# The norm of the last two tokens taken apart from its half, with their residual sums in four column groups

## The chip, the cores and the metric

One core of a Trainium2 chip runs the whole program. The metric is the device time of one execution in microseconds (us). The kernel before has a median of 1541.15 us over three runs (1540.23 to 1541.41).

## The reference

A block with a token mixer and a gated channel mixer, for 1024 tokens behind 16 learned ones (T = 1040), model width 1024, 2816 inner channels, all in float32:

```
h = concat(meta, x)
h = h + token_mixer(rmsnorm(h, norm_mix_g))        # eight heads, then "mixed @ w_out"
u = rmsnorm(h, norm_ffn_g)
h = h + (silu(causal_dwconv(u @ w_up)) * (u @ w_gate)) @ w_down
out = rmsnorm(h, norm_final_g)[:, 16:]

def rmsnorm(x, g):
    return x * rsqrt(mean(x * x, axis=-1) + EPS) * g
```

The mixer is four mLSTM heads and four retention heads, each worked in chunks of tokens with a state that is carried on.

## The kernel before, in words

Activations lie channel by token: `resid` has 128 partitions, 8 blocks of channels and 1040 columns (tokens). Every float32 product is made of three matmuls of 32-bit "fp32r" operands: each operand is split into `hi` (a rounded copy, on ACT) and `lo` (the rest, on DVE), and hi·hi, hi·lo and lo·hi are added in PSUM. Lines 394 to 396, 404 to 406 and 577 to 579 are such triples. A scheduler of the framework turns the program text into one fixed order for each engine, and each engine then works strictly in that order; dependences between engines are semaphore waits. PSUM has eight banks, handed out by tags: `pp` (3), `sA` (2), `num`, `upd` and `tr` (1 each).

**Heads.** `ORDER` puts head 4 (`HF`) first. For each head `o_group` makes the gates, then `v_group` of the next head runs chunk by chunk while the scan of this head (`scan_a`, `scan_b`) is woven in. Weights come through `need(key, ahead)`, which loads and splits units in a fixed sequence: v, v, q, k, o, o of one head, then of the next. `ahead` says how many units further the split is issued; line 442 asks for 4 in the second half of `o_group`, so the next head's q weights are split (lines 162 and 163, `hi_q` on ACT, `lo_q` on DVE) from there. For q units the split is ordered behind the latest evacuation of a v chunk (`last["v"]`). The raw weights have a ring of two buffers.

**The output projection.** `mixw` multiplies by `w_out` with a seven-product scheme over steps named 1, 65, 73, 4 and 2. It covers columns 14 to 1037. The last two tokens (columns 1038 and 1039) are kept apart: DVE accumulates their product in `acc` (`last_two`), with channels along the free dimension, as partial sums over 128 partitions. Inside step 4, line 1216 sums them over the partitions and turns them to channel by token: 16 matmuls, one for each channel block and token, with a piece of `acc` as weights and one column of ones as the moving operand. Line 1217 adds the result to `resid`.

**The norms behind it.** `norm_tasks` squares each channel block (line 1122, ACT), sends the block to a DRAM copy (`stream`, line 1124, SP) and adds the squares up in `Rb` (line 1126, DVE). `rms` sums over the partitions (line 314, PE, tile `pcb`), takes root and reciprocal (lines 319 and 320) and spreads the factor to all partitions (line 325, PE, `prb`); line 329 (ACT) copies it to `Rb`. `scale_tasks` multiplies `resid` by it (line 1136, DVE) and writes the split operands `xh` and `xl` (lines 1064 and 1065). The second half of the tokens, columns 526 to 1039, is one unit of 514 columns (`BQ`), so its squares stand behind line 1217. Its norm has one sum bank and one broadcast bank, both of tag `tr`; as 514 is two more than four times 128, it has a small group of two columns and four of 128.

**Step 2 and the quarters.** Step 2 fills four banks `pwy` for the first quarter of the tokens; line 736 (DVE) adds each to `resid`. Then the same four banks are filled for the second quarter, with operands `wl`; each of these starts when line 736 has read its bank. Behind them come the first up and gate products (`first_up`, `first_gate`, tiles `pup` and `pga`), the second half of the tokens first.

Of the kernel before, what the change touches and what calls it, by code (L numbers as in the profile page):

```python
# [10 lines left out]
F32 = mybir.dt.float32  # L11
# [52 lines left out]
def body(ctx, tc, h_in, vecs, cst, mask_in, rot, w_v0, w_v, w_fm, w_out, w_up, w_gate, w_down, out):  # L64
# [46 lines left out]
    def pp(name, tag="pp"):  # L111
        return ps.tile([P, 512], F32, tag=tag, name=name, bufs=PSB[tag])
# [193 lines left out]
    def rms(ss, t0, t1, nm, col, rb, ptags=("tr", "num"), more=(), sq=None):  # L306
        n = t1 - t0
        o = n % P
        subs = ([(0, o)] if o else []) + [(i, P) for i in range(o, n, P)]
        ns = len(subs)  # L310
        pc = rps("pc" + nm, ptags[0])
        for i, (o, w) in enumerate(subs):
            for a in (ss, *more):
                nc.tensor.matmul(pc[:w, i:i + 1], a[:, o:o + w], cs[:, C_M01 + P - 1:C_M01 + P], start=a is ss, stop=a is (ss, *more)[-1])
        i0 = 1 if subs[0][1] < P else 0
        for w, j0, j1 in ([(subs[0][1], 0, 1)] if i0 else []) + [(P, i0, ns)]:
            if sq is not None:
                nc.vector.tensor_scalar(sq[:w, j0:j1], pc[:w, j0:j1], 1.0 / D, EPS, ALU.mult, ALU.add)
            nc.scalar.activation(col[:w, j0:j1], pc[:w, j0:j1], AF.Sqrt, bias=epsc[:w], scale=1.0 / D)
            nc.vector.reciprocal(col[:w, j0:j1], col[:w, j0:j1])  # L320
        pr = rps("pr" + nm, ptags[1])
        x = max(0, n - 512)
        for i, (o, w) in enumerate(subs):
            dst = pr[:, o - x:o - x + w] if o >= x else pc[:, 8:8 + w]
            nc.tensor.matmul(dst, col[:w, i:i + 1].to_broadcast([w, P]), ident[:w, :w], start=True, stop=True)
        if x:
            nc.scalar.copy(rb[:, :x], pc[:, 8:8 + x])
        if rb is not None:
            nc.scalar.copy(rb[:, x:], pr[:, :n - x])
        return pr[:, :n - x]  # L330
# [107 lines left out]
    def o_group(h, b, p):  # L438
        t0, t1, _ = PIECES[p]
        t0 = max(t0, KEEP)  # L440
        n = t1 - t0
        U = need(("o", h, b), 4 if b and p and h != 7 else 2)
        pt = pp(f"po{h}_{b}_{p}")
        fm_mms(pt, U, t0, t1)
        s = sig(b, p)
        nc.vector.tensor_tensor(s, pt[:, :n], Rb[:, t0:t1], ALU.mult)
        x = nc.scalar.activation(s, s, AF.Sigmoid if h < H else AF.Silu)
        if h < H:
            after(x, last["silu"])
        last["gate"] = x  # L450
# [120 lines left out]
    def mm3s(pt, a, x, first, last):  # L571

        n = len(a)
        m = []
        for k in range(n):
            (ah, al), (xh_, xl_) = a[k], x[k]
            m.append(nc.tensor.matmul(pt, ah, xh_, start=first and k == 0, stop=False, skip_group_check=True))  # L577
            nc.tensor.matmul(pt, ah, xl_, start=False, stop=False, skip_group_check=True)  # L578
            m.append(nc.tensor.matmul(pt, al, xh_, start=False, stop=last and k == n - 1, skip_group_check=True))  # L579
        return m[0], m[-1]  # L580
# [21 lines left out]
    class Seven:  # L602
# [120 lines left out]
        def last_quarter(self, i, done):  # L723

            st = self.order[-1]
            T0 = 4 * self.kn
            b = "xy"[st == "2"]
            if i:
                r = [self.late.pop(k, None) or self.rhalf(k, 1) for k in range(self.kn)]
            for j in range(4):  # L730
                pt = self.banks[b, j][:, i * QT:(i + 1) * QT]
                if i:
                    mm3s(pt, [tuple(y[:, j * P:(j + 1) * P] for y in self.ops[T0 + k][0][0]) for k in range(self.kn)], r, st == "2", True)
                m = j + 4 * (st == "4")
                x = resid[:, m, self.base + i * QT:self.base + (i + 1) * QT]
                V.tensor_tensor(x, pt, x, ALU.add)
                done(m)
# [317 lines left out]
    def xb(i):  # L1055
        return blocks[i]
# [15 lines left out]
    def ftile(nm):  # L1072
        return fp.tile([P, XW + 2], F32, tag="f", name=nm, bufs=5)
# [42 lines left out]
    def norm_tasks(t0, t1, mbs=range(KB), first=True):  # L1116
        n = t1 - t0
        ss = Rb[:, t0:t1]

        def one(mb):  # L1120
            dst = ss if first and mb == mbs[0] else (ftile(f"sqb{t0}_{mb}") if n > HB else fp.tile([P, QT], F32, tag="sqb", name=f"sqb{t0}_{mb}", bufs=2))[:, :n]
            nc.scalar.activation(dst, resid[:, mb, t0:t1], AF.Square)
            u0 = max(t0, META)
            nc.sync.dma_start(stream[:, mb, u0 - META:t1 - META], resid[:, mb, u0:t1])
            if not (first and mb == mbs[0]):
                V.tensor_tensor(ss, ss, dst, ALU.add)
        return [lambda mb=mb: one(mb) for mb in mbs]

    def scale_tasks(t0, t1, tag):
        def norm():  # L1130
            col = tmp.tile([P, 5], F32, tag="rcol", name=f"rcolb{t0}")
            rms(Rb[:, t0:t1], t0, t1, f"b{t0}", col, Rb[:, t0:t1], ptags=(tag, tag))

        def one(kb):
            x = resid[:, kb, t0:t1]
            V.tensor_tensor(x, x, Rb[:, t0:t1], ALU.mult)
            last["scaled"] = xsingle(kb, t0, TA + XW if t1 == TB else t1, t0 >= TB)
        return [norm] + [lambda kb=kb: one(kb) for kb in range(KB)]
# [37 lines left out]
    def fblock(b):  # L1176
        return tuple(fp.tile([P, 4, XW], F32R, name=f"x{x}{b}", tag=f"x{x}{b}", bufs=1) for x in "hl")

    BQ, AQ = [(MB, T)], [(MA, MA + QT), (MA + QT, MB)]
    side = []  # L1180

    def some(n):
# [3 lines left out]
    for t, (st, k) in enumerate(mixw.steps):  # L1186
        if st == "2":
            break
        if t == 0:
            mixw.pump()  # L1190
        if st == "65" and k == 1:
# [12 lines left out]
        if t == KW - 1:  # L1204
            mixw.mms(t)
        for u in range(t, min(t + (3 if st == "4" or (st, k) == ("73", KW - 1) else 2), 4 * KW)):
            mixw.prep(u)
            if mixw.steps[u][0] == "73" and u % 2 and u + 7 not in mixw.four:
                mixw.pre4(u + 7)
        if t != KW - 1:  # L1210
            mixw.mms(t)
        if st == "4" and k == 0:
            pe = pp("pe2", "tr")
            for mb in range(KB):
                for i in range(2):
                    nc.tensor.matmul(pe[:, 2 * mb + i:2 * mb + i + 1], acc[:, i, mb * P:(mb + 1) * P], cs[:, C_M01 + P - 1:C_M01 + P], start=True, stop=True)
            V.tensor_tensor(resid[:, :, T - 2:], pe[:, :2 * KB].rearrange("p (m i) -> p m i", i=2), resid[:, :, T - 2:], ALU.add)
# [412 lines left out]
```

## Time and profile before

| What | Value |
|---|---|
| median of three runs | 1541.15 us |
| the profiled execution's own time | 1539.83 us |
| its span, first to last instruction | 1537.7 us |
| PE busy | 1517.2 us (99%) |
| DVE busy | 1090.8 us (71%) |
| ACT busy | 722.7 us (47%) |
| granted TensorE clock, mean | 0.999 |

About 2.1 us of the execution lie around the span. Rows of the timeline read: start, duration, engine, line, operation, out<-in, shapes, count, and in brackets how long the engine stood idle before it and what released it. A matmul's duration overlaps the next one's; the distance between starts is what a matmul takes of PE's time. A float32 matmul that isn't split shows as two records. Where engines stand in the order is shown below in rows of the engines' programs, which have no times.

### The profile page before, as it was taken

To read this page: it belongs to the slowest core of one execution; us is meant where nothing else is said; L and a number is where in the kernel's file an instruction comes from. 1 tells how busy PE (TensorE), PEld (TensorE's weight loads), DVE (VectorE), ACT (ScalarE), POOL (GpSimd) and SP (SyncE) were. 2 spreads that over 40 slices of the span, in tenths; PEclk is the share of its full clock that TensorE was granted. 3 is DMA by queue.
4 is the path that set the end of the run, shared out by engine and by line. 5 is a ranking of instruction groups with operands and counts; after the bars stand their busy time and mean duration, and the time that the engine had idled before them with its cause. 6 is when DMAs were issued, how large, how long until landed. Compare 5 with 4: busy or idle time off the path is not lost.

```text
span 1537.7 us, 25392 instructions
## 1 busy us (share of the span) xinstructions
PE 1517.2 (99%) x9763; PEld 1394.6 (91%) x9763; DVE 1090.8 (71%) x2334; ACT 722.7 (47%) x1480; POOL 101.2 (7%) x117
## 2 busy tenths in 40 slices
PE   8999999999999999999999999999999999999997
PEld 7989999999999999997788998999999999888887
DVE  8757667676867575679967788677666666778657
ACT  7355554555543434336454465444444445344443
POOL 0000001010010000000000000212101110000000
PEclk9999999999999999999999999999999999999999
DMA  6122425352556334346543237888666667933313
GB/s 230 56 70 90 110 90 124 116 122 88 142 136 161 77 110 90 109 96 242 178 140 107 83 110 252 207 214 204 158 155 154 148 153 202 366 106 107 96 42 110
DMA packets 105192, 213.41 MB, mean 139 GB/s; under 512 B 9384, under 2 KB 31600, under 8 KB 105072
## 3 DMA queue, kind: packets, MB, share of 16 engines
q1 hardware_dynamic: 86384, 176.86, 34.1%
q0 software_dynamic: 18544, 34.87, 15.1%
q8 instruction: 76, 1.25, 0.3%
q14 instruction: 44, 0.36, 0.1%
q10 hardware_dynamic: 144, 0.07, 0.0%
HBM read 182.37 MB, written 84.19 MB: 173 GB/s over the span
## 4 chain that ended last, share of the span: by engine, by line
PE 96%; ACT 1%; DVE 1%; DMA 1%; issue 0%; SPq 0%; DVEq 0%
PE pv L394 4%; PE pv L395 4%; PE po L404 4%; PE po L406 4%; PE po L405 4%; PE pv L396 4%; PE pdx L577 3%; PE pdx L579 3%; PE pdx L578 3%; PE pup_x L578 2%; PE pup_x L579 2%; PE pga_x L577 2%; PE pga_x L579 2%; PE pga_x L578 2%; PE pup_x L577 2%; PE pdy L577 2%
## 5 line engine op out<-in xcount | busy, mean ns | idle before, releaser
L394 PE MATMUL pv<-hi_v,uh 128*128 128x256 f32 (+1 forms) x512 | 147.4, 288 | 2.6 <-ACT hi_v L162 1.6
L396 PE MATMUL pv<-hi_v,ul 128*128 128x256 f32 (+1 forms) x512 | 145.1, 284 | 0.0
L395 PE MATMUL pv<-lo_v,uh 128*128 128x256 f32 (+1 forms) x512 | 145.1, 284 | 0.0
L404 PE MATMUL po<-uh,hi_o 128*128 128x386 f32 (+2 forms) x384 | 124.1, 323 | 0.0
L405 PE MATMUL po<-ul,hi_o 128*128 128x386 f32 (+2 forms) x384 | 122.6, 319 | 0.0
L406 PE MATMUL po<-uh,lo_o 128*128 128x386 f32 (+2 forms) x384 | 122.6, 319 | 0.0
L394 PEld LDWEIGHTS pv<-hi_v,uh 128*128 128x128 f32 x512 | 97.4, 190 | 6.3 <-issue 2.9
L395 PEld LDWEIGHTS pv<-lo_v,uh 128*128 128x128 f32 x512 | 97.2, 190 | 0.8 <-DVE lo_v L163 0.8
L396 PEld LDWEIGHTS pv<-hi_v,ul 128*128 128x128 f32 x512 | 97.0, 190 | 0.1
L212 POOL DMA_DIRECT2D wsd<-w_down_d x55 | 50.9, 1025 | 571.8 <-DMA wsd<-w_down_d 474.4
L261 ACT CAST hi_up<-raw_up 128x512 fp32r<-128x512 f32 (+1 forms) x52 | 36.5, 720 | 106.6 <-PE pga_z L578 61.2
L404 PEld LDWEIGHTS po<-uh,hi_o 128*128 128x128 f32 x384 | 72.4, 189 | 0.2
L406 PEld LDWEIGHTS po<-uh,lo_o 128*128 128x128 f32 x384 | 72.3, 188 | 0.1
L405 PEld LDWEIGHTS po<-ul,hi_o 128*128 128x128 f32 x384 | 72.3, 188 | 0.1
L262 DVE TENSOR_TENSOR lo_ga<-fraw_ga,hi_ga 128x512 fp32r<-128x512 f32 (+1 forms) x52 | 41.9, 809 | 37.8 <-ACT hi_ga L261 37.6
L577 PE MATMUL pup_x<-uh_g,hi_up 128*128 128x256 f32 (+1 forms) x240 | 67.2, 282 | 0.4 <-ACT uh_g L1061 0.4
L578 PE MATMUL pup_x<-ul_g,hi_up 128*128 128x256 f32 (+1 forms) x240 | 67.4, 283 | 0.1
L262 DVE TENSOR_TENSOR lo_up<-raw_up,hi_up 128x512 fp32r<-128x512 f32 (+1 forms) x52 | 41.4, 810 | 35.6 <-ACT hi_up L261 34.8
L579 PE MATMUL pup_x<-uh_g,lo_up 128*128 128x256 f32 (+1 forms) x240 | 66.3, 282 | 0.0
L212 POOL DMA_DIRECT2D wsw<-w_out_d x40 | 37.2, 1028 | 402.0 <-DMA wsw<-w_out_d 362.6
L404 PE MATMUL pq<-uh,hi_q 128*128 128x400 f32 (+2 forms) x192 | 62.6, 326 | 0.2 <-DVE rq L425 0.2
L405 PE MATMUL pk<-ul,hi_k 128*128 128x400 f32 (+2 forms) x192 | 62.2, 324 | 0.0
(751 smaller groups left out, 5040.8 us busy)
## 6 DMA issues: line engine op xcount, KB each, us to landing
raw_up<-w_up_d SPq DMA_DIRECT2D x22, 512.0 KB, 5.7
fraw_ga<-w_gate_d SPq DMA_DIRECT2D x22, 512.0 KB, 4.0
acts<-cv SPq DMA_DIRECT2D x44, 256.0 KB, 5.7
wsd<-w_down_d SPq DMA_DIRECT2D x22, 512.0 KB, 6.3
wsd<-w_down_d POOLq DMA_DIRECT2D x22, 512.0 KB, 6.6
rd<-wsd SPq DMA_DIRECT2D x22, 512.0 KB, 3.5
wsd<-w_down_d POOLq DMA_DIRECT2D x33, 256.0 KB, 6.8
raw_o<-w_fm_d SPq DMA_DIRECT2D x16, 512.0 KB, 3.5
```

Source lines behind the costliest of these rows:

```text
L212: nc.gpsimd.dma_start(x, v, accum_op=ALU.add)
L261: nc.scalar.copy(hi[:, o:o + n], x)
L262: nc.vector.tensor_tensor(lo[:, o:o + n], x, hi[:, o:o + n].bitcast(F32), ALU.subtract)
L394: nc.tensor.matmul(pv[:L, :nv], a, hi[:, o:o + nv], start=kb == 0, stop=False)
L395: nc.tensor.matmul(pv[:L, :nv], a, lo[:, o:o + nv], start=False, stop=False)
L396: nc.tensor.matmul(pv[:L, :nv], b, hi[:, o:o + nv], start=False, stop=kb == KB - 1)
L404: nc.tensor.matmul(pt[:, :n], a, uh[kb][:, t0:t1], start=kb == 0, stop=False)
L405: nc.tensor.matmul(pt[:, :n], a, ul[kb][:, t0:t1], start=False, stop=False)
L406: nc.tensor.matmul(pt[:, :n], b, uh[kb][:, t0:t1], start=False, stop=kb == KB - 1)
L577: m.append(nc.tensor.matmul(pt, ah, xh_, start=first and k == 0, stop=False, skip_group_check=True))
L578: nc.tensor.matmul(pt, ah, xl_, start=False, stop=False, skip_group_check=True)
L579: m.append(nc.tensor.matmul(pt, al, xh_, start=False, stop=last and k == n - 1, skip_group_check=True))
```

## The change

Five edits:

1. In head 4's `o_group`, line 442, the look-ahead of 4 becomes 2, as for head 7. The next head's q split is then issued by `v_group`.
2. The two tokens' sums are made with `acc` as the moving operand: eight matmuls of 256 columns, four column groups of the array side by side (`tile_position`), with a 32-column selector `pick` as weights. ACT copies the result back into `acc`, two PE transposes turn it to channel by token, and DVE adds it to `resid` in two instructions. The transposes stand one step later (k = 1).
3. The second half's norm covers 512 columns; its sum bank has tag `num` and its broadcast bank `tr`.
4. The two tokens get a norm and a scaling of their own, `two()`, queued behind the second half's: one square of 16 columns, one DMA to `stream` in 1024 pieces of 8 bytes, three small additions, a sum and a broadcast of two columns (banks `sA`), two small multiplications, and the split into the last two columns of the operand tiles.
5. The first up product is ordered behind the last matmul of the quarters (`last["end"]`).

```diff
-        U = need(("o", h, b), 4 if b and p and h != 7 else 2)
+        U = need(("o", h, b), 4 if b and p and h not in (HF, 7) else 2)
...
-                    mm3s(pt, [tuple(y[:, j * P:(j + 1) * P] for y in self.ops[T0 + k][0][0]) for k in range(self.kn)], r, st == "2", True)
+                    last["end"] = mm3s(pt, [tuple(y[:, j * P:(j + 1) * P] for y in self.ops[T0 + k][0][0]) for k in range(self.kn)], r, st == "2", True)[1]
...
+    def two():
+        x, R = resid[:, :, T - 2:], Rb[:, T - 2:]
+        t = ftile("sq2")[:, :2 * KB].rearrange("p (k t) -> p k t", t=2)
+        nc.scalar.activation(t, x, AF.Square)
+        nc.sync.dma_start(stream[:, :, SEQ - 2:], x)
+        for n in (4, 2, 1):
+            V.tensor_tensor(t[:, :n], t[:, :n], t[:, n:2 * n], ALU.add)
+        rms(t[:, 0], T - 2, T, "b2", tmp.tile([P, 5], F32, tag="rcol", name="rcolb2"), R, ptags=("sA", "sA"))
+        V.tensor_tensor(x, x, R.rearrange("p (o t) -> p o t", o=1).to_broadcast([P, KB, 2]), ALU.mult)
+        V.tensor_tensor(t, x, vec[:, V_FFN:V_FFN + KB].rearrange("p (k o) -> p k o", o=1).to_broadcast([P, KB, 2]), ALU.mult)
+        for i, k in ((6, 0), (2, 4)):
+            hi, lo = (y[:, :, XW - 2:] for y in xb(i))
+            nc.scalar.copy(hi, t[:, k:k + 4])
+            V.tensor_tensor(lo, t[:, k:k + 4], hi.bitcast(F32), ALU.subtract)
...
-    BQ, AQ = [(MB, T)], [(MA, MA + QT), (MA + QT, MB)]
+    BQ, AQ = [(MB, T - 2)], [(MA, MA + QT), (MA + QT, MB)]
...
+        if st == "4" and k == 0:
+            pe, n = pp("pe2", "tr"), D // 4
+            for i in range(2):
+                for j in range(4):
+                    nc.tensor.matmul(pe[32 * j:32 * j + 32, :n], pick[:, i, :], acc[:, i, j * n:(j + 1) * n], start=i == 0, stop=i == 1, tile_position=(0, 32 * j))
+            nc.scalar.copy(acc[:, 0, :n], pe[:, :n])
         if t != KW - 1:
             mixw.mms(t)
-        if st == "4" and k == 0:
-            pe = pp("pe2", "tr")
-            for mb in range(KB):
-                for i in range(2):
-                    nc.tensor.matmul(pe[:, 2 * mb + i:2 * mb + i + 1], acc[:, i, mb * P:(mb + 1) * P], cs[:, C_M01 + P - 1:C_M01 + P], start=True, stop=True)
-            V.tensor_tensor(resid[:, :, T - 2:], pe[:, :2 * KB].rearrange("p (m i) -> p m i", i=2), resid[:, :, T - 2:], ALU.add)
+        if st == "4" and k == 1:
+            for i in range(2):
+                y = pe[:, D // 4 + i * P:D // 4 + (i + 1) * P]
+                nc.tensor.transpose(y, acc[:, 0, i * P:(i + 1) * P], ident)
+                x = resid[:, i:KB:2, T - 2:]
+                V.tensor_tensor(x, y.rearrange("p (j t) -> p j t", t=32)[:, :, 0:2], x, ALU.add)
...
-                side += norm_tasks(*BQ[0]) + scale_tasks(*BQ[0], "tr")
+                side += norm_tasks(*BQ[0]) + scale_tasks(*BQ[0], "num", "tr") + [two]
...
-            some(100)
```

The changed kernel's program has the following lines in place of those of before: 1136 is now 1151, 1216 is 1233 (with the transposes at 1240 and the additions at 1242); `two()` is lines 1129 to 1142.

**ACT in the first head's v stage.** The rows are ACT's program around the q split; `kwh`, `pt`, `qd` and `S` are operands of the scan, `vh` the evacuation of a v chunk, each followed by its chunk's number. Before:

```order
L838 ACTIVATE kwh_2_1091<-s_2_1087,Rc 128x128
L808 CAST pt_2h<-pt_2_1089 128x128
L162 CAST hi_q_0_1127<-raw_q_0_1125 128x1024
L838 ACTIVATE kwh_3_1168<-s_3_1164,Rc 128x128
L808 CAST pt_3h<-pt_3_1166 128x128
L808 CAST qd_3h<-qT 128x128
L880 COPY num_0_1033<-n_1_1108 128x256
L369 ACTIVATE vh<-pv_1_1292,Rc 128x256
L369 ACTIVATE vh<-v_0_1276,Rc 16x256
L808 CAST S_1h<-C_1_1116 128x256
```

Now the same stretch, further down to the q split:

```order
L369 ACTIVATE vh<-pv_2_1325,Rc 128x256
L838 ACTIVATE kwh_5_1356<-s_5_1352,Rc 128x128
L808 CAST pt_5h<-pt_5_1354 128x128
L808 CAST qd_5h<-qT 128x128
L880 COPY num_0_1033<-n_3_1238 128x256
L808 CAST S_3h<-C_3_1246 128x256
L369 ACTIVATE vh<-pv_3_1392,Rc 128x256
L162 CAST hi_q_0_1495<-raw_q_0_1255 128x1024
L838 ACTIVATE kwh_6_1423<-s_6_1419,Rc 128x128
```

`hi_q` stood behind the scan's chunk 2 and ahead of chunk 3; now it stands behind the evacuation of v chunk 3 and ahead of the scan's chunk 6. `lo_q` moves alike on DVE. SP's order of loads is the same there.

**DVE behind step 4.** The rows are DVE's program from the last evacuation of step 4 on; `pwx` and `pwy` are banks of `w_out`, `Rb` the sums and then the norm's factor. Before:

```order
L721 TENSOR_TENSOR resid<-resid,pwx_8888 128x512
L1126 TENSOR_TENSOR Rb<-Rb,sqb_5_10030 128x256
L587 TENSOR_TENSOR rr_8822<-wa_8851,rr_8822 128x256
L587 TENSOR_TENSOR rr_8822<-wa_8765,rr_8822 128x256
L1126 TENSOR_TENSOR Rb<-Rb,sqb_6_10034 128x256
L320 RECIPROCAL rcolb_9738<-rcolb_9738 2x1
L320 RECIPROCAL rcolb_9738<-rcolb_9738 128x4
L1126 TENSOR_TENSOR Rb<-Rb,sqb_7_10038 128x256
L1136 TENSOR_TENSOR resid<-resid,Rb 128x514 x8
L736 TENSOR_TENSOR resid<-pwy_9864,resid 128x256
L736 TENSOR_TENSOR resid<-pwy_9868,resid 128x256
L736 TENSOR_TENSOR resid<-pwy_9872,resid 128x256
```

Now (the half's reciprocal has moved up, ahead of these rows):

```order
L721 TENSOR_TENSOR resid<-resid,pwx_8892 128x512
L587 TENSOR_TENSOR rr_8822<-wa_8851,rr_8822 128x256
L587 TENSOR_TENSOR rr_8822<-wa_8765,rr_8822 128x256
L1126 TENSOR_TENSOR Rb<-Rb,sqb_5_10045 128x256
L1151 TENSOR_TENSOR resid<-resid,Rb 128x512 x8
L320 RECIPROCAL rcolb_9825<-rcolb_9825 2x1
L1126 TENSOR_TENSOR Rb<-Rb,sqb_6_10049 128x256
L736 TENSOR_TENSOR resid<-pwy_9887,resid 128x256
L1065 SCALAR_TENSOR_TENSOR xl_9650<-resid,vec,xh_9649 128x512 x4
L1065 SCALAR_TENSOR_TENSOR xl_9648<-resid,vec,xh_9647 128x512
L736 TENSOR_TENSOR resid<-pwy_9891,resid 128x256
```

The two tokens' reciprocal (`2x1`) now stands behind the eight multiplications of the half. The first three `pwy` evacuations stood in one row; now five `xl` rows stand between the first and the second.

**PE at the two tokens' broadcast.** Before, it stood inside step 2, between matmuls of a bank's sixth to eighth operand:

```order
L577 MATMUL pwy_9872<-rr_8822,wl_9852 128x256
L578 MATMUL pwy_9872<-rr_8822,wl_9852 128x256
L325 MATMUL pcb_9739<-cs,rcolb_9738 128x2
L579 MATMUL pwy_9872<-rr_8822,wl_9853 128x256
L577 MATMUL pwy_9864<-wr_00_9856,wl_9920 128x256
```

Now it stands between the second and the third bank, which are filled one after the other:

```order
L577 MATMUL pwy_9891<-rr_8822,wl_9935 128x256
L578 MATMUL pwy_9891<-rr_8822,wl_9935 128x256
L579 MATMUL pwy_9891<-rr_8822,wl_9936 128x256
L325 MATMUL prb_9830<-cs,rcolb_9825 128x2
L577 MATMUL pwy_9879<-wr_00_9871,wl_9867 128x256
L578 MATMUL pwy_9879<-wr_00_9871,wl_9867 128x256
```

Ahead of it PE has, in this order: the half's sums (`pcb`, four records' pairs) within step 4, 32 matmuls of 512 columns and one of the two transposes, six of `pwy`, the half's broadcast (`prb`), four of `pwy`, the two tokens' sum, and 38 of `pwy`. Three `pup` matmuls that stood ahead of the second quarter's `pwy` now stand behind them.

More of the change, by code (lines that the diff above doesn't have):

```diff
@@ L315, in rms @@
         i0 = 1 if subs[0][1] < P else 0
-        for w, j0, j1 in ([(subs[0][1], 0, 1)] if i0 else []) + [(P, i0, ns)]:
+        for w, j0, j1 in ([(subs[0][1], 0, 1)] if i0 else []) + ([(P, i0, ns)] if i0 < ns else []):
             if sq is not None:
@@ L1120, in one @@
         def one(mb):
-            dst = ss if first and mb == mbs[0] else (ftile(f"sqb{t0}_{mb}") if n > HB else fp.tile([P, QT], F32, tag="sqb", name=f"sqb{t0}_{mb}", bufs=2))[:, :n]
+            dst = ss if first and mb == mbs[0] else (ftile(f"sqb{t0}_{mb}") if n > QT else fp.tile([P, QT], F32, tag="sqb", name=f"sqb{t0}_{mb}", bufs=2))[:, :n]
             nc.scalar.activation(dst, resid[:, mb, t0:t1], AF.Square)
@@ L1125, in one, with scale_tasks @@
             if not (first and mb == mbs[0]):
-                V.tensor_tensor(ss, ss, dst, ALU.add)
+                last["sq"] = V.tensor_tensor(ss, ss, dst, ALU.add)
         return [lambda mb=mb: one(mb) for mb in mbs]
-    def scale_tasks(t0, t1, tag):
+    def two():
[12 more added lines that the diff above has]
+            V.tensor_tensor(lo, t[:, k:k + 4], hi.bitcast(F32), ALU.subtract)
+    def scale_tasks(t0, t1, *tags):
         def norm():
             col = tmp.tile([P, 5], F32, tag="rcol", name=f"rcolb{t0}")
-            rms(Rb[:, t0:t1], t0, t1, f"b{t0}", col, Rb[:, t0:t1], ptags=(tag, tag))
+            rms(Rb[:, t0:t1], t0, t1, f"b{t0}", col, Rb[:, t0:t1], ptags=(tags[0], tags[-1]))
         def one(kb):
@@ L1190, in body @@
             mixw.pump()
+            pick = ftile("pick")[:, :64].rearrange("p (t j) -> p t j", t=2)
+            nc.gpsimd.memset(pick, 0.0)
+            for i in range(2):
+                nc.gpsimd.memset(pick[:, i, i:i + 1], 1.0)
         if st == "65" and k == 1:
@@ L1209, in body @@
                 mixw.pre4(u + 7)
+        if st == "4" and k == 0:
[4 more added lines that the diff above has]
+            nc.scalar.copy(acc[:, 0, :n], pe[:, :n])
         if t != KW - 1:
             mixw.mms(t)
-        if st == "4" and k == 0:
-            pe = pp("pe2", "tr")
-            for mb in range(KB):
-                for i in range(2):
-                    nc.tensor.matmul(pe[:, 2 * mb + i:2 * mb + i + 1], acc[:, i, mb * P:(mb + 1) * P], cs[:, C_M01 + P - 1:C_M01 + P], start=True, stop=True)
-            V.tensor_tensor(resid[:, :, T - 2:], pe[:, :2 * KB].rearrange("p (m i) -> p m i", i=2), resid[:, :, T - 2:], ALU.add)
+        if st == "4" and k == 1:
+            for i in range(2):
+                y = pe[:, D // 4 + i * P:D // 4 + (i + 1) * P]
+                nc.tensor.transpose(y, acc[:, 0, i * P:(i + 1) * P], ident)
+                x = resid[:, i:KB:2, T - 2:]
+                V.tensor_tensor(x, y.rearrange("p (j t) -> p j t", t=32)[:, :, 0:2], x, ALU.add)
         if st == "4":
@@ L1316, in eight @@
             pt = bank(m)[:, :j1 - j0]
+            end = last.pop("end", None)
             xs = [xb(kb // 4 if half == 0 else (6, 2)[kb // 4]) for kb in range(KB)]
-            mm3s(pt, [tuple(y[:, kb * P:(kb + 1) * P] for y in (hi, lo)) for kb in range(KB)],
-                 [tuple(y[:, kb % 4, j0:j1] for y in xs[kb]) for kb in range(KB)], True, True)
+            x = mm3s(pt, [tuple(y[:, kb * P:(kb + 1) * P] for y in (hi, lo)) for kb in range(KB)],
+                     [tuple(y[:, kb % 4, j0:j1] for y in xs[kb]) for kb in range(KB)], True, True)
+            if end:
+                after(x[0], end)
             done(m, pt)
```

## The prediction

> **What bounds the kernel now.** The page first: PE is busy for all but 20 us of the span, and the chain of work that ended last runs on PE for 96% of it.
>
> ```profile
> span 1537.7 us, 25392 instructions
> ...
> PE 1517.2 (99%) x9763; PEld 1394.6 (91%) x9763; DVE 1090.8 (71%) x2334; ACT 722.7 (47%) x1480; POOL 101.2 (7%) x117
> ...
> PE 96%; ACT 1%; DVE 1%; DMA 1%; issue 0%; SPq 0%; DVEq 0%
> ```
>
> So only two things can move the end: what PE itself is given to do, and what PE waits for. The list of PE's waits comes next (total, times, longest). Of its rows these lie where the change works:
>
> ```profile
> PE u L846 <- ACT vh L369: 1.7, 1, 1.7
> ...
> PE pwy L577 <- DVE resid L736: 0.9, 1, 0.9
> ...
> PE n L846 <- ACT num L880: 0.8, 1, 0.8
> ...
> PE pup_x L577 <- ACT uh_g L1061: 0.4, 1, 0.4
> ...
> PE pq L404 <- DVE rq L425: 0.2, 1, 0.2
> ```
>
> The first belongs to edit 1, the second to edits 2 to 4. The others stand downstream of those places: they say how much of a gain may be lost again, or added.
>
> **Edit 1, the later q split.** The timeline of the first head's v stage:
>
> ```profile
> 92.34 0.35 SPq L146 DMA_DIRECT2D raw_q<-w_fm_d  x1
> ...
> 99.61 1.05 ACT L162 CAST hi_q<-raw_q 128x1024 fp32r<-128x1024 f32 x1 [4.33 <-DMA raw_q<-w_fm_d]
> ...
> 100.69 1.28 DVE L163 TENSOR_TENSOR lo_q<-raw_q,hi_q 128x1024 fp32r<-128x1024 f32 x1 [3.88 <-ACT hi_q L162]
> ...
> 102.47 0.51 ACT L369 ACTIVATE vh<-v,Rc 16x256 fp32r<-16x256 f32 x1 [0.51 <-DVE v L388]
> ...
> 103.03 0.35 PE L846 MATMUL u<-vh,kwh 128*128 128x256 f32 x1 [1.70 <-ACT vh L369]
> ...
> 109.27 0.30 ACT L808 CAST pt_5h<-pt 128x128 fp32r<-128x128 f32 x1 [2.13 <-PE n L847]
> 109.48 0.47 ACT L369 ACTIVATE vh<-pv,Rc 128x256 fp32r<-128x256 f32 x1
> ```
>
> ACT stands at `hi_q` until its load lands, 4.33 us, and DVE behind ACT at `lo_q`, 3.88 us; everything queued behind them (the next `kwh`, `vh`, the state `C`) is late, and PE pays 1.70 us. Now the split stands behind the `vh` at 109.48. SP issues the load where it did, so it has landed some 10 us before ACT comes to it. The two instructions (1.05 and 1.28 us) are then plain work; what covers them is ACT's idle time there (2.13 us ahead of 109.27). Were that cover gone, the next `kwh` and `kwl` would be up to 1.3 us late, and part of that could reach PE. I take the whole wait as gone: **−1.7**, bounds 0 (the next operand is late by as much) and −2.5 (the 0.8 at `num` goes as well).
>
> **Edit 2, the sums.** Rows of PE: the old sums and the matmul behind them, and two groups of the kind that the new code uses (four column groups of 32, 256 columns, two records each):
>
> ```profile
> 821.15 3.63 PE L1216 MATMUL pe<-cs,acc 128*128 128x1 f32 x32
> 824.64 0.48 PE L578 MATMUL pwx<-rr,w4xh 128*128 128x512 f32 x1
> ...
> 184.15 0.64 PE L383 MATMUL pv<-raw_v,ug 128*32 128x256 f32 x8
> ...
> 268.85 1.06 PE L383 MATMUL pv<-raw_v,ug 128*32 128x256 f32 x12
> ```
>
> The old sums take 824.64 − 821.15 = 3.5 of PE's time (3.63 with the tail). The new ones are eight matmuls, two rounds of four groups. Four cost 0.64, six cost 1.06; eight cost between 1.06 and 2 × 0.64 = 1.28, I take 1.2, and with tails on both sides 3.63 − 1.2 gives **−2.4** (−2.3 to −2.6). [...]
>
> Two transposes are added. A float32 transpose alone, between matmuls of 384 columns:
>
> ```profile
> 138.60 0.34 PE L404 MATMUL pq<-uh,hi_q 128*128 128x384 f32 x1
> 138.78 0.27 PE L926 MATMUL tr<-cs,num 128*128 128x128 f32 x1
> 139.06 0.34 PE L406 MATMUL pq<-uh,lo_q 128*128 128x384 f32 x1
> ...
> 139.41 0.34 PE L405 MATMUL pq<-ul,hi_q 128*128 128x384 f32 x1
> ```
>
> With it in between, two starts lie 0.46 apart, without it 0.35: 0.11 each, at most its 0.27. Two: **+0.2** (0.2 to 0.5). The ACT copy and the two additions on DVE have 26 matmuls of 512 columns between the sums and the first transpose in PE's order, some 6 us (0.12 for 256 columns, below); PE waits for neither. `pick` is filled by POOL over 100 us ahead.
>
> **Edits 3 and 4, the norms.** What the second half's norm does now, in rows of all engines, from the last evacuations on:
>
> ```profile
> 817.95 2.56 ACT L587 CAST wl<-wa 128x256 fp32r<-128x256 f32 x8 [3.87 <-DVE rr L587]
> ...
> 824.82 0.17 DVE L1217 TENSOR_TENSOR resid<-pe,resid 128x16 f32<-128x16 f32 x1 [2.47 <-PE pe L1216]
> ...
> 825.03 0.64 ACT L1122 ACTIVATE Rb<-resid 128x514 f32<-128x514 f32 x1 [3.48 <-DVE resid L1217]
> ...
> 837.30 0.68 DVE L721 TENSOR_TENSOR resid<-resid,pwx 128x512 f32<-128x512 f32 x1
> ...
> 838.23 1.88 DVE L721 TENSOR_TENSOR resid<-resid,pwx 128x512 f32<-128x512 f32 x3
> ...
> 839.10 0.28 PE L577 MATMUL pwy<-wr,wl 128*128 128x256 f32 x1
> 839.22 0.28 PE L578 MATMUL pwy<-wr,wl 128*128 128x256 f32 x1
> ...
> 840.02 1.17 PE L314 MATMUL pcb<-cs,Rb 128*2 128x1 f32 x10
> ...
> 840.36 0.75 DVE L587 TENSOR_TENSOR rr<-wa,rr 128x256 fp32r<-128x256 f32 x2
> ...
> 847.42 1.05 PE L325 MATMUL prb<-cs,rcolb 128*128 128x128 f32 x8
> 848.23 0.36 PE L579 MATMUL pwy<-rr,wl 128*128 128x256 f32 x1
> 848.51 0.59 ACT L329 COPY Rb<-prb 128x512 f32<-128x512 f32 x1 [3.45 <-PE prb L325]
> 849.12 4.92 DVE L1136 TENSOR_TENSOR resid<-resid,Rb 128x514 f32<-128x514 f32 x8 [6.97 <-ACT Rb L329]
> ...
> 853.96 1.08 DVE L736 TENSOR_TENSOR resid<-pwy,resid 128x256 f32<-128x256 f32 x3
> ...
> 854.44 0.38 PE L577 MATMUL pwy<-wl,wl 128*128 128x256 f32 x1 [0.93 <-DVE resid L736]
> ```
>
> PE waits 0.93 us at 854.44 for a bank that L736 empties, and L736 stands behind the eight multiplications of 849.12 to 854.04, which wait for the broadcast at 847.42. What moves is that broadcast. Squares needn't wait for the two tokens (the 3.48 us at 825.03), so by the order the half's sum lies inside step 4 and its broadcast six matmuls into step 2. Five of the eight squares (0.64 at most each) now stand ahead of ACT's row at 817.95, in its 3.87 us of idle time. On this profile's clock, edit 1 left aside: step 2 starts at 839.10 − 2.4 + 0.2 + 0.8 (four fifths of the `pcb` row, now ahead of it) = 837.7; the broadcast, 6 × 0.12 later, at 838.4. From its start to the first multiplication the rows have 849.12 − 847.42 = 1.7, which gives 840.1. DVE's own queue sets the rest: in the rows above, its work from 837.30 ends at 841.11, 3.8 us; shifted by −1.4 and lengthened by the three additions of `two()` (0.17 each) and one of the half, it comes to 840.5. The multiplications end at 845.4, and L736 follows. The second quarter starts on PE near 852, so its first two banks are long empty: **−0.9**, no bound above it but 0.
>
> A wait is added. The two tokens' reciprocal now stands behind the eight multiplications on DVE, and PE's broadcast of these two columns waits for it: ready at 845.5. PE is there at 838.4 + 0.8 (the half's broadcast, 848.23 − 847.42) + 42 × 0.12 + 0.3 (the two-token sum) = 844.5. Behind it on PE's queue are two banks of the first quarter and all of the second: a wait is lost time. I take **+1.0**, bounds 0 and +2. The small groups of two columns were there before as a part of the five-group rows; as groups of their own **+0.1**.
>
> Also new: one square and one copy on ACT, six small operations on DVE, all beside PE's 99%; and a DMA of 1024 pieces on SP, issued near 835.5, for which the two tokens' multiplication waits on DVE near 852. Behind that wait stand the last two L736, whose banks the second quarter needs at about 855.5. At nothing, if it lands within some 17 us.
>
> **Edit 5** moves three `pup` matmuls behind the quarters. PE's work stays, and nobody waits for them: 0.
>
> **Sum**: −1.7 − 2.4 + 0.2 + 0.1 − 0.9 + 1.0 = −3.7. The profiled execution's 1539.83 becomes 1536.1. It lies 1.3 below the median of the runs, so the median becomes 1537.4. About 0.2%, 3.1 us, is what a measurement of this kernel can tell from no change: faster means below 1538.1, slower above 1544.2.
>
> **Rivals.**
>
> *The early gain is handed on.* The scan's `n` waits 0.8 for `num` and the next stage 0.2 for `rq` further down; and 1.05 + 1.28 us of split now stand in front of a later `kwh`. If such a wait takes 1.7 us back, edit 1 is worth 0 and the time is 1539.1: the same. For it speaks that ACT and DVE do as much work as before. Against it, that they stood idle for 4.33 and 3.88 us, and that this idle time goes. Chance 0.14.
>
> *The two tokens' broadcast becomes the stall.* If the multiplications begin 1 to 1.5 us later (`Rb` is copied by ACT, where squares wait for the last evacuations), PE waits 2 to 2.5 there and not 1.0: 1538.4 to 1538.9, the same. Chance 0.13.
>
> *More goes than the sum counts.* The 0.8 and the 0.4 at `pup_x` vanish too, or the new wait is 0: 1535.2 to 1536.2. Chance 0.10.
>
> *The small pieces land late, and it is slower.* The DMA of 1024 pieces of 8 bytes has no like in this trace:
>
> ```profile
> A<-scr SPq DMA_DIRECT2D x8, 512.0 KB, 5.2
> ...
> resid<-h_in_d SPq DMA_DIRECT2D x2, 1024.0 KB, 12.4
> ```
>
> The nearest row lands after 5.2 us, the longest after 12.4. DVE waits for it ahead of the two tokens' multiplication, with L736 behind. It costs from about 17 us after its issue; every microsecond beyond is PE's. To cancel 3.7 and be slower by 3.1, it must take 17 + 6.8 = 24 us or more: 1544.3. [...] Nothing else waits for it before the end. Chance 0.04.
>
> **How the numbers follow.** Forecast 0.59, with 1537.4; on its own, by the bounds of the new wait (0 to 2) and of the sums, 1536.2 to 1538.5. The two rivals that end on no change reach 1539.1; both at once give 1540.5. The range is 1535.2 to 1539.8. Faster: 0.10, and of the forecast's 0.59 all but 0.03, which is 0.56: 0.66. Same: 0.14 + 0.13 + 0.03 = 0.30. Slower: 0.04.
>
> **What would show it.** In the changed kernel's profile: `hi_q` without a wait for its DMA, and no 1.7 at u L846 (if another row of PE's waits has grown by as much, the first rival is right). The row of the sums near 1.2. A row "PE prb L325 <- DVE rcolb" with about 1.0, and none for pwy L577 behind L736. The multiplications starting some 8 us sooner before the second quarter than now. The multiplication in `two()` on DVE not waiting for the DMA. PE's busy sum lower by about 2.1. Wrong would be: a PE that is busy as long as before, or a new wait of over 2 us behind the two tokens.

## The result, and the profile after

The changed kernel takes 1535.51 us (median of six executions, 1534.86 to 1536.01) against 1541.28 for the kernel before, run beside it: a ratio of 0.9962 (0.9951 to 0.9972). Two later series gave 0.9958 (0.9944 to 0.9972) and 0.9960 (0.9947 to 0.9972). It is 5.8 us faster; the forecast was 3.8, with 1535.2 as the low end of the range. The profiled execution took 1536.01, 3.8 us less than that of before. The page of the changed kernel:

```profile
span 1534.2 us, 25396 instructions
...
PE 1516.1 (99%) x9749; PEld 1392.2 (91%) x9749; DVE 1094.6 (71%) x2342; ACT 723.4 (47%) x1484; POOL 101.5 (7%) x120
...
PE 97%; DVE 1%; ACT 1%; DMA 0%; issue 0%; DVEq 0%; ACTq 0%
```

PE still bounds the kernel. The list of PE's waits, at the places that the prediction named:

```profile
PE n L846 <- ACT num L880: 0.7, 1, 0.7
...
PE pup_x L577 <- ACT uh_g L1061: 0.4, 1, 0.4
PE prb L325 <- DVE rcolb L320: 0.4, 1, 0.4
...
PE pq L404 <- DVE rq L425: 0.2, 1, 0.2
```

The 1.7 at u L846 and the 0.9 at pwy L577 are gone. The three waits downstream are as long as they were, to 0.1. One row is new, the 0.4 at the two tokens' broadcast.

**Edit 1.** The first head's v stage, timeline of all engines:

```profile
99.88 0.28 PE L846 MATMUL u<-vh,kwh 128*128 128x256 f32 x1
...
107.83 1.04 ACT L162 CAST hi_q<-raw_q 128x1024 fp32r<-128x1024 f32 x1
...
109.26 1.20 DVE L163 TENSOR_TENSOR lo_q<-raw_q,hi_q 128x1024 fp32r<-128x1024 f32 x1
```

`hi_q` has no bracket any more: ACT doesn't stand still for the load, and the `u` matmul doesn't wait. Much later the gain is still there. A landmark near the end of the heads, the last `u` of the scan's fifth chunk, then a `pwx` row behind it; first before, then after:

```profile
691.61 0.35 PE L846 MATMUL u<-vh,kwh 128*128 128x256 f32 x1 [0.29 <-DVE mv L915]
...
702.26 1.10 PE L577 MATMUL pwx<-rr,hi_w 128*128 128x512 f32 x4
```

```profile
689.69 0.36 PE L846 MATMUL u<-vh,kwh 128*128 128x256 f32 x1 [0.30 <-DVE mv L915]
...
701.39 1.09 PE L577 MATMUL pwx<-rr,hi_w 128*128 128x512 f32 x4
```

At the first landmark the changed kernel is 1.92 ahead, at the second only 0.87. Between them 1.05 is lost. The same stretch in windows of 2 us (length, busy time of each engine, then granted clock, DMA share, GB/s) shows to what:

```profile
692.00:694.00 2.00, 1.81 (x8) 1.35 (x7) 1.85 (x5) 2.00 (x6) 0.00 (x0) 0.78 0.96 358
694.00:696.00 2.00, 2.00 (x8) 1.77 (x9) 1.23 (x4) 1.97 (x3) 0.00 (x0) 0.50 1.02 379
696.00:698.00 2.00, 2.00 (x10) 1.48 (x8) 2.00 (x4) 0.99 (x5) 0.00 (x0) 0.87 1.02 375
```

The granted clock falls to half, 0.50 in the middle window; at half, the three windows make (0.22 + 0.50 + 0.13) x 2 / 0.5 = 3.4 us. In the profile of before it is 1.00 there. Such a drop isn't a part of the change's sum; what it has to do with the change is a question for the experiments.

**Edit 2.** The sums with the matmuls of 512 columns around them. Of before, the matmul ahead of the old sums (821.15 to 824.64) and the second one behind them:

```profile
820.92 0.39 PE L577 MATMUL pwx<-rr,w4xh 128*128 128x512 f32 x1
...
824.96 0.39 PE L579 MATMUL pwx<-rr,w4xl 128*128 128x512 f32 x1
```

Of after, and further on the first transpose:

```profile
820.17 0.40 PE L577 MATMUL pwx<-rr,w4xh 128*128 128x512 f32 x1
820.50 1.07 PE L1233 MATMUL pe<-acc,pick 128*32 128x256 f32 x16
...
821.50 0.50 PE L578 MATMUL pwx<-rr,w4xh 128*128 128x512 f32 x1
821.84 0.39 PE L579 MATMUL pwx<-rr,w4xl 128*128 128x512 f32 x1
...
827.40 0.40 PE L579 MATMUL pwx<-wr,w4xl 128*128 128x512 f32 x1
827.63 0.27 PE L1240 MATMUL pe<-cs,acc 128*128 128x128 f32 x1
827.66 0.48 PE L577 MATMUL pwx<-wr,w4xh 128*128 128x512 f32 x1
...
827.97 0.39 PE L578 MATMUL pwx<-wr,w4xh 128*128 128x512 f32 x1
```

From its own start to the next one's the row takes 821.50 - 820.50 = 1.00 where it took 3.49. But the matmul ahead of the new sums takes 0.33 and not its usual 0.23, and the one behind them 0.34 (behind the old ones 0.32). From matmul to matmul, less 0.46 for the two of 512 columns, the old sums cost 824.96 - 820.92 - 0.46 = 3.58 and the new ones 821.84 - 820.17 - 0.46 = 1.21: a gain of 2.37. From 827.40 to 827.97 two matmuls take 0.57, without a transpose 0.46 (twice 0.23): 0.11 for a transpose, 0.23 for both.

**Edits 3 and 4.** The half's norm and the two tokens':

```profile
837.12 0.28 PE L577 MATMUL pwy<-wr,wl 128*128 128x256 f32 x1
...
837.82 1.05 PE L325 MATMUL prb<-cs,rcolb 128*128 128x128 f32 x8
...
838.91 0.59 ACT L329 COPY Rb<-prb 128x512 f32<-128x512 f32 x1 [0.20 <-PE prb L325]
...
839.53 4.91 DVE L1151 TENSOR_TENSOR resid<-resid,Rb 128x512 f32<-128x512 f32 x8 [0.18 <-ACT Rb L329]
...
844.35 0.14 DVE L320 RECIPROCAL rcolb<-rcolb 2x1 f32<-2x1 f32 x1
...
844.55 0.38 PE L325 MATMUL prb<-cs,rcolb 2*128 2x2 f32 x2 [0.38 <-DVE rcolb L320]
...
850.61 0.28 PE L577 MATMUL pwy<-wl,wl 128*128 128x256 f32 x1
...
851.05 0.16 DVE L1137 TENSOR_TENSOR resid<-resid,Rb 128x16 f32<-128x16 f32 x1
```

The second quarter's first matmul (850.61) follows without a wait. It comes 11.1 us behind the start of the multiplications, before it was 5.3. The two tokens' multiplication has no bracket: the DMA of small pieces, which it had to wait for, landed after 2.8 us.

```profile
stream<-resid SPq DMA_DIRECT2D x1, 8.0 KB, 2.8
```

The span's balance: 1.92 + 2.37 + 0.93 gained; 0.23 + 0.38 lost; 4.6 in all. Take off the 1.05 of the clock and 0.12 more by which the lead had shrunk between 701 and 820 us (0.87 to 820.92 - 820.17 = 0.75), and 3.4 is left; the spans (1537.7 and 1534.2) differ by 3.5.

### The profile page after: what moved, and what is told of

It is laid out like the page before. It is cut to its first block, busy times and chain, and to the rows that moved or that the text cites. A ratio compares the mean times of both kernels' runs of the same rounds, so it can differ in the third digit from the quotient of the medians.

```text
span 1534.2 us, 25396 instructions
## 1 busy us (share of the span) xinstructions
PE 1516.1 (99%) x9749; PEld 1392.2 (91%) x9749; DVE 1094.6 (71%) x2342; ACT 723.4 (47%) x1484; POOL 101.5 (7%) x120
## 4 chain that ended last, share of the span: by engine, by line
PE 97%; DVE 1%; ACT 1%; DMA 0%; issue 0%; DVEq 0%; ACTq 0%
PE pv L394 4%; PE pv L395 4%; PE pv L396 4%; PE po L404 4%; PE po L406 4%; PE po L405 4%; PE pdx L577 3%; PE pdx L579 3%; PE pdx L578 3%; PE pup_x L578 2%; PE pup_x L579 2%; PE pup_x L577 2%; PE pga_x L577 2%; PE pga_x L579 2%; PE pga_x L578 2%; PE pq L404 2%
## 5 line engine op out<-in xcount | busy, mean ns | idle before, releaser
L577 PE MATMUL pup_x<-uh_g,hi_up 128*128 128x256 f32 (+1 forms) x240 | 67.3, 282 | 0.4 <-ACT uh_g L1061 0.4
```

## The experiments

Twelve runs, three of them of the two kernels unchanged, each timed beside the kernel before on its own chip (medians of before 1541.13, 1541.48 and 1540.97 in the three series). Ratios are to it.

### Both kernels once more

> The kernel before once more, unchanged. The two profiled executions differ by 3.5 us of span, the medians by 5.8. Theory: the terms of the sum are real and constant (4.6 us), and the rest is the granted clock, which fell to about half for 4 us in the profile of after (693 to 697 us) and not in that of before. Then the median here is 1541 again, and where a profile of before has such a stretch its span is about 1 us longer than 1537.7. Rival: the clock never falls there in before; its span is then 1537.7 again with no such stretch.

> The changed kernel once more, unchanged. Theory: a median near 1535.5; in the profile the same waits as before (0.4 at the two tokens' broadcast, none at u L846); the stretch with the lower clock may be there or not, worth about 1 us of the span: 1533.2 without it, 1534.2 with it. Rival: the stretch belongs to the changed kernel's order and shows again at the same place.

> The changed kernel once more, on the same chip as the three others, as the base for their differences: 1535.4, with 0.4 at the two tokens' broadcast.

Before: 1541.19, ratio 0.9999 (0.9989 to 1.0009), span 1537.7 again and no drop of the clock in the profile: for the profile the rival was right. After: 1535.26 and 1535.18. Its profiles differ: the first repetition has drops at 34 and 692 us and a span of 1534.8, the second at 8 and 34 us and 1533.4. So the drop at 692 comes and goes with one and the same order, and a profile is one draw. Over all fourteen profiles here a drop near that place (690 to 698) is in seven and in neither of before's; that the changed order makes it likelier is not excluded. (Every profile also ends with the clock at half, for 4 to 9 us; that stretch is left out here, but it is in the mean of an execution.) Each execution comes with its mean granted clock, and these, a rough measure, can be counted:

| Mean granted clock | before: executions, median | after: executions, median |
|---|---|---|
| 0.993 or lower | 21, 1543.9 | none |
| 0.994 to 0.995 | 22, 1541.4 | 1, 1536.5 |
| 0.996 | 14, 1540.4 | 11, 1535.3 |
| 0.997 or higher | 28, 1539.9 | 4, 1534.8 |

At an equal clock the difference is 4.8 to 5.1, near the 4.6 of the rows (the 4.8 rests on one execution of after). The medians differ by more, 5.8; a quarter of before's executions have a clock that no execution of after had. The profile of before is one of its best.

### Edit 1 alone, and all but edit 1

The first run has the kernel before with the new line 442 and nothing else, the second the changed kernel with the old line 442.

> The kernel before with edit 1 alone (look-ahead 2 in head 4). Theory: the wait of 1.7 us at u L846 goes and no other takes its place: 1.9 us less than before, 1539.3. Rival (first rival of the prediction): another wait takes it back, 1541.2.

> The changed kernel without edit 1 (look-ahead 4 again). Theory: the 1.7 us wait is back and nothing else changes: 1535.5 + 1.9 = 1537.4, with the waits at the quarters as in the changed kernel (0.4 at the two tokens' broadcast, none at pwy L577 behind L736). Rival: edit 1 is worth more than its wait (the median moved by 5.8, the terms make 4.6), 1538.5 or more.

Alone: 1539.95, 1.2 below its before, ratio 0.9989 (0.9978 to 0.9999). Undone in the changed kernel: 1537.43, ratio 0.9977 (0.9968 to 0.9987), 2.2 above after's 1535.26. Where edit 1 is undone, the wait is back, and in this execution the clock drops right behind it (windows of 2 us):

```profile
103.20 0.36 PE L846 MATMUL u<-vh,kwh 128*128 128x256 f32 x1 [1.82 <-ACT vh L369]
```

```profile
104.00:106.00 2.00, 2.00 (x12) 2.00 (x11) 2.00 (x8) 1.03 (x3) 0.00 (x0) 0.50 0.45 182
106.00:108.00 2.00, 2.00 (x14) 2.00 (x13) 0.92 (x4) 0.28 (x2) 0.00 (x0) 0.65 0.00 0
```

In the run with edit 1 alone the old sums are still there, and in its profile a drop follows on them:

```profile
819.66 3.63 PE L1216 MATMUL pe<-cs,acc 128*128 128x1 f32 x32
```

```profile
824.00:826.00 2.00, 2.00 (x7) 1.57 (x6) 1.18 (x2) 2.00 (x5) 0.00 (x0) 0.61 0.84 315
826.00:828.00 2.00, 2.00 (x6) 1.55 (x5) 1.79 (x4) 2.00 (x5) 0.00 (x0) 0.54 1.01 379
```

Edit 1 is worth its wait, as far as the times can tell: 1.2 and 2.2 lie on both sides of the 1.92 of the rows, and the interval of the first only just leaves out no change. No other wait took it back. Where edit 1 is undone, one more wait is longer in this profile, 0.9 at `pwx` L577 behind ACT where after has 0.2, in a stretch with another drop (698 us).

### Edit 2 alone, and all but edit 2

The first has the kernel before with the diff's new sums, transposes and `pick`, the second the changed kernel with the old lines:

```diff
         if t != KW - 1:
             mixw.mms(t)
+        if st == "4" and k == 0:
+            pe = pp("pe2", "tr")
...
+                    nc.tensor.matmul(pe[:, 2 * mb + i:2 * mb + i + 1], acc[:, i, mb * P:(mb + 1) * P], cs[:, C_M01 + P - 1:C_M01 + P], start=True, stop=True)
```

> The kernel before with edit 2 alone: the new sums and transposes, the norm of the second half still over 514 columns, so that its squares stand behind the second addition of the sums (834.3 in the changed kernel, where the old squares began at 825.0). Theory: edit 2 saves its 2.3 us of PE only where the norm doesn't wait for it; here the broadcast of the half moves later, not earlier, and PE waits at the quarters or at the first up products for 1.5 us or more: 1540.4 or above, against 1541.1 before. Rival (each edit is worth its own term, alone as together): 1541.1 - 2.3 = 1538.8, with the 0.9 at pwy L577 as before.

> The changed kernel with the old sums (16 matmuls of one column at the old place) and all else as changed. Theory: the row of the sums is 3.6 again and not 1.07, the two transposes go, and the two tokens' norm comes earlier, so that its 0.4 us wait goes: 1535.4 + 2.5 - 0.2 - 0.4 = 1537.3. Rival: the order changes more than that (the half's eight multiplications now stand ahead of step 4's last evacuations and of the last splits of rr on DVE), and PE waits there for 1 us or more: 1538.5 or above.

Edit 2 alone: 1538.69, ratio 0.9981 (0.9973 to 0.9990), 2.8 below before. My theory fell; the rival held in the median, though not in its detail. The half's multiplications do start later (853.15, before 849.12), as I had argued. But the scheduler answers: three of the bank evacuations now stand ahead of them on DVE, and PE's wait at pwy L577 behind L736 is gone too.

```profile
847.91 1.11 DVE L736 TENSOR_TENSOR resid<-pwy,resid 128x256 f32<-128x256 f32 x3 [0.65 <-PE pwy L579]
...
853.15 4.91 DVE L1136 TENSOR_TENSOR resid<-resid,Rb 128x514 f32<-128x514 f32 x8
```

The price comes further on, in two of PE's waits that grew by 0.8 each against before:

```profile
PE pup_x L577 <- ACT uh_g L1061: 1.2, 1, 1.2
...
PE pga L577 <- ACT hi_ga L261: 0.8, 1, 0.8
```

So of the gain from the sums on, 2.37 - 0.23 + 0.93 - 1.6 = 1.5 is left by the rows; the median moved by 2.8, with executions at 0.995 to 0.998 and none as low as 0.993. The split norm (edits 3 and 4) then buys back the 1.6 for its 0.4.

The changed kernel with the old sums: 1542.88, ratio 1.0006 (0.9996 to 1.0017), 7.6 above after. Theory had 1537.3; the rival was right, and by more than it said. The half's broadcast comes earlier there, and the scheduler puts the eight multiplications ahead of step 4's last evacuations and of the last splits of `rr`:

```profile
838.54 4.91 DVE L1151 TENSOR_TENSOR resid<-resid,Rb 128x512 f32<-128x512 f32 x8 [2.78 <-ACT Rb L329]
...
849.16 0.75 DVE L587 TENSOR_TENSOR rr<-wa,rr 128x256 fp32r<-128x256 f32 x2
...
849.63 0.39 PE L578 MATMUL pwy<-rr,wl 128*128 128x256 f32 x1 [3.27 <-DVE rr L587]
```

PE waits 3.27 for the split. With 2.37 for the sums, less 0.23 and 0.38, that makes 5.0; its profile has drops of the clock behind both places (822 and 850 us), and its executions go down to 0.991. This run therefore tells less of the sums than of the order: as the scheduler orders them, edits 3 and 4 without the new sums lose at least what edit 1 gains, since this kernel is no faster than before.

### The wait that was left

> The changed kernel with the sum, reciprocal and broadcast of the two tokens queued ahead of the half's multiplications, and only their scaling behind (a second small tile for the products, so that the two parts don't share one). The two tokens' reciprocal then stands behind three of the eight multiplications on DVE and not behind all. Theory: the 0.4 us wait at the broadcast goes and no other comes: 1535.4 - 0.4 = 1535.0. Rival: PE only waits a little later for the banks that DVE empties later: 1535.4, with a row at pwy L577.

> The changed kernel without edit 5. Two first up products then stand right ahead of the two tokens' broadcast on PE. Theory: they fill 0.24 of the 0.38 us wait, and nobody waits for the banks that they take: 1535.4 - 0.2 = 1535.2, with 0.1 at the broadcast; edit 5 is worth nothing or a little loss. Rival: edit 5 carries a part of the gain that the sum doesn't count (the medians moved by 5.7, the terms make 4.6): 1536.5.

> The changed kernel with the two tokens' norm queued ahead of the half's multiplications and without edit 5, both together. Theory: each of the two alone removes the same 0.4 us wait, so together they are worth no more than one: 1534.8, as either alone. Rival: edit 5 costs something of its own beside that wait: 1534.3 or less.

The first queues the two tokens' norm ahead of the half's multiplications (`two()` cut in two behind `rms`), the second leaves out edit 5, the third does both:

```diff
-                side += norm_tasks(*BQ[0]) + scale_tasks(*BQ[0], "num", "tr") + [two]
+                sc2 = scale_tasks(*BQ[0], "num", "tr")
+                side += norm_tasks(*BQ[0]) + sc2[:1] + [two_norm] + sc2[1:] + [two]
...
-            if end:
-                after(x[0], end)
```

1534.68, 1534.97 and 1535.07; ratios 0.9950 (0.9938 to 0.9962), 0.9953 (0.9940 to 0.9966), 0.9956 (0.9943 to 0.9970). In none of the three profiles is there a row for the broadcast. In the first the reciprocal stands behind three multiplications, and PE comes to its broadcast 2.6 us after it is done:

```profile
838.12 1.90 DVE L1155 TENSOR_TENSOR resid<-resid,Rb 128x512 f32<-128x512 f32 x3 [0.19 <-ACT Rb L329]
...
839.94 0.14 DVE L320 RECIPROCAL rcolb<-rcolb 2x1 f32<-2x1 f32 x1
...
842.70 0.38 PE L325 MATMUL prb<-cs,rcolb 2*128 2x2 f32 x2
```

All three medians lie 0.1 to 0.6 below after's on the same chip, where 0.2 to 0.4 was expected, and their intervals overlap with its: the times don't resolve it. The traces do. From the start of the two tokens' sums to the first down product (`pdx`), the three profiles of after take 483.24 to 483.27 us, these three 482.89, 483.05 and 482.84: 0.36, 0.20 and 0.41 less, as each was expected. Both together are worth little more than one. Edit 5 brings nothing: it takes away the two matmuls that would fill the wait. The first is the best of all kernels here by its median, and clearly below before.

### What a stretch with little work costs

> The changed kernel with 16 matmuls of one column (the form of the old sums, on constants, into a bank that nobody reads) early in the output projection. The order on all engines behind it stays as it is. In the profiles so far the granted clock falls to half for some 3.4 us right behind a stretch in which PE waited or had little to do: at 104 behind the 1.7 us wait, at 822 to 827 behind the old sums, at 850 behind a wait of 3.3, at 692 behind the transposes. Theory: such a stretch costs more than its own length, because the drop behind it costs another 1 us or so in the executions that have it; 3.5 + 0.5 to 1.5, so 1539.4 to 1540.4, with a drop behind the new row in the profile. Rival: it costs its own 3.5 us, 1538.9, and no drop follows.

> As the run with 16 one-column matmuls, at the same place of PE's order, with 8 matmuls of 128 x 256 in place of them, which keep the array busy for about as long (4 times 0.117 us each by the row of 256 columns for a product that is split in three: some 3.5 to 4 us; the profile's distance between starts is taken). Theory: the cost is that distance and no drop of the clock follows behind the row. Rival: the drop comes wherever something is put in, or at random: the cost beyond the row's own length is the same as in the other run.

```diff
+        if st == "1" and k == 3:
+            dm = pp("dm", "tr")
+            for i in range(16):
+                nc.tensor.matmul(dm[:, i:i + 1], cs[:, :P], cs[:, C_M01 + P - 1:C_M01 + P], start=True, stop=True)
```

The other has `range(8)`, output `dm[:, :2 * P]` and moving operand `cs[:, :2 * P]`. The row put in, the matmul behind it, and the windows there; the one-column matmuls first:

```profile
732.14 3.83 PE L1240 MATMUL dm<-cs 128*128 128x1 f32 x32 [0.79 <-DVE mm L933]
735.84 0.78 PE L577 MATMUL pwy<-wr,hi_w 128*128 128x512 f32 x1
```

```profile
736.00:738.00 2.00, 2.00 (x5) 1.61 (x6) 0.26 (x1) 0.00 (x0) 0.00 (x0) 0.50 0.00 0
738.00:740.00 2.00, 2.00 (x8) 1.54 (x8) 0.00 (x0) 0.00 (x0) 0.00 (x0) 0.75 0.03 8
```

And the matmuls of 256 columns:

```profile
732.50 3.69 PE L1240 MATMUL dm<-cs 128*128 128x256 f32 x16 [0.80 <-DVE mm L933]
735.84 1.05 PE L577 MATMUL pwy<-wr,hi_w 128*128 128x512 f32 x3
```

```profile
736.00:738.00 2.00, 2.00 (x10) 1.62 (x10) 0.61 (x1) 0.00 (x0) 0.00 (x0) 1.00 0.00 0
```

From start to start the rows take 3.70 and 3.34. (A matmul of 256 columns that isn't split takes 3.34 / 8 = 0.42 of PE's time here, 3.6 times the 0.117 of one of a split product; the 4 times of the expectation was the author's estimate.) The kernels take 1545.08, ratio 1.0028 (1.0019 to 1.0037), and 1540.43, ratio 0.9993 (0.9984 to 1.0002): 9.9 and 5.25 above after on the same chip. The order behind the row did not stay as it was: PE's next matmuls differ in the two kernels and from after's, and each has one more wait in the profile, 0.7 and 0.5.

In the profiles the drop can be priced. Nine matmuls of 512 columns behind the first row take 3.62 (735.84 to 739.46) where they take 2.1 at full clock: 1.5. From the pair of transposes ahead of the row to the two tokens' sums, PE takes 6.35 more than in the second repetition of after with the first row and 4.62 more with the second. Row, wait and drop make 5.9 of the 6.35, row and wait 3.8 of the 4.62; the rest, 0.4 and 0.8, I take for the order.

In the profiles the two kernels differ by 1.7, in the medians by 4.65. Seven of the eleven executions of the first kernel have a clock of 0.991 to 0.993 and a median of 1546.1, the other four 0.995 and 1543.5; the second has 0.995 or 0.996 in all. But at the same 0.995 the second's seven executions have a median of 1540.4, 3.0 less, so the mean clock does not explain all of the difference, and what is left of it I can't name. The theory's direction is shown: the drop follows on the one-column row and not on the other. Its size was too small: 9.9 where 4.0 to 5.0 was expected, and 5.25 where the row's 3.34 was.

Apart from the stretch at the end, every drop in these profiles makes some 3.4 us at half by the windows of 2 us, and drops come and go between executions. One followed on a wait of 1.82 us (edit 1 undone), one on a row of one-column matmuls for which the timeline gives PE no idle time (edit 1 alone, 819.66). What sets their length, and why one execution has one and another none, no run here shows.

## Why the prediction was right, and where its sizes were off

The direction and the places were right, and most terms were within 0.2. That the number lies in the range is in part luck. The measured 1535.51 is outside what the forecast gave on its own (1536.2 to 1538.5) and in the band of the rival *More goes than the sum counts*, whose conditions did not come: the 0.8 and the 0.4 at `pup_x` stayed, and the new wait was not 0. What carried it there were 0.9 us by which the sum was too small, and the drops of the clock, which the prediction did not have.

- **What bounds it**: right. Only PE's work, PE's waits and PE's clock moved the end; DVE and ACT do slightly more than before.
- **Edit 1, -1.7**: measured -1.92 at the landmark. No wait downstream grew, so the first rival is out.
- **The sums, -2.4**: -2.37. The new ones cost 1.2, as written, but made up otherwise: the row lasts 1.07, the next start comes after 1.00, and 0.1 lies ahead of it and 0.1 behind. The prediction's row of 0.64 has such a part beside it too (from the matmul at 183.94 to the row at 184.15 are 0.21 us, where its neighbours take 0.12). The 32 old records took 3.49 / 32 = 109 ns each, for one column with 128 columns of weights, little less than the 0.117 us of a matmul of 256 columns of a split product. What sets that price is not shown: no run here changes the weights alone.
- **Transposes, +0.2, and small groups, +0.1**: 0.23, and nothing: the sums over the partitions cost the same 1.22 us of PE before and after.
- **The stall at the quarters, -0.9**: gone. One step was argued wrongly: the multiplications were not held by DVE's own queue. The row at 839.53 names ACT's copy, 1.7 behind the broadcast's start, as the other path had it.
- **The new wait, +1.0**: 0.38. Right in its place and cause, mis-sized: the reciprocal came 0.3 sooner (by that other path), and PE came there 0.3 later than the count of matmuls gave. This is the largest error of the sum. With 0.2 at edit 1 and 0.1 at the small groups put right, the sum would have been -4.6.
- **The DMA of 8-byte pieces**: 2.8 us, below the nearest row (5.2) and far from the 24 that the slower rival needed, and DVE's multiplication at 851.05 did not wait for it. What the size of the pieces alone does to that time, no run shows.
- **From the profile to the median**: the step that was missing. I set the sum against the profiled execution and moved it to the median as if the clock were the same in all. The gaps that the change closes, a wait of 1.7 and 3.5 us of one-column matmuls, are of the kind behind which the clock dropped in some profiles (to half at 104 and at 824 us), and closing them would save the drops too. By the table the clock makes 0.7 to 1.0 of the 5.8. That a drop can follow on a stretch of one-column matmuls is shown by the pair with 1 and 256 columns (0.50 and 1.00 from 736 to 738 us, in one profile each); for a wait there are two profiles (1.82 and 3.27 us) and no pair. That it was these two places which made before's executions of 0.993 is argued, from the two profiles in which a drop follows on just these rows. The count over all kernels fits it. At 0.993 or lower are 21 of 85 executions with both the old sums and the wait (before), 1 of 12 with the old sums alone (edit 1 alone; 4 of 12 in the changed kernel with the old sums, which has a wait of 3.27 of its own), 2 of 24 with the wait alone (edit 2 alone, edit 1 undone), and none of 33 with neither (after, and the three kernels without the 0.4 wait). But a drop of 3.4 us at half clock is only 0.0011 of a mean, so such an execution has several: the one profile taken at 0.993 has drops at 8, 36, 104 and 698 us, of which these two places explain one.
- **Signs to look for**: PE's busy sum fell by 1.1 and not 2.1, since matmuls last longer at half clock and count as busy (0.63 us and not 0.39 for 512 columns, in the drop at 824 us with edit 1 alone); in the second repetition, without the drop at 692, it is 1514.4, 2.8 less than before. The lead of the multiplications grew by 5.8, not 8.

## What to carry to other kernels

When one engine is busy for 99%, add up only its own work and its waits; rows of a like form price a new form well, and a wait made from two paths is worth the later path, so time both. Ask of each order that a scheduler makes what it puts ahead of what: edit 2 alone and edits 3 and 4 without it did other things than their parts of the sum. And compare several executions with their granted clocks before a difference of 1 us is given to an edit: a profile is one draw.

## What the runs showed of the hardware

- The granted clock fell to half for some 3.4 us behind a short stretch in which PE waited (1.82 us and 3.27 us, one profile each) or ran matmuls of one column (rows of 3.63 and 3.83 us), in some executions and not in others: the profile of before has a wait of 1.70 us and the old row of 3.63 and no drop behind either. A drop cost 1.05 us in one place and, under full load, 1.5 in two others (nine matmuls of 512 columns from 824.39 to 828.03 in the run with edit 1 alone, and from 735.84 to 739.46 in that with one-column matmuls put in, where they take 2.1).
- 16 one-column matmuls put into the kernel cost 9.9 us, 8 matmuls of 256 columns 5.25 at the same place, though their rows take 3.70 and 3.34; the traces account for 6.35 and 4.62.
- Eight matmuls in two rounds of four column groups, 32 x 256 each, took 1.2 us of PE: 1.00 for the row and 0.1 on either side of it.
- A DMA of 1024 pieces of 8 bytes landed in 2.8 us.
